# Hybrid decoder trunk: first modulation by blocks of 128 channels on TensorE, the first gate with it, sine tables early

## The chip, the cores and the metric

The kernel runs on one core of one Trainium2 chip. The metric is the device time of one execution in microseconds (us); the input arrays are laid out on the host beforehand and that does not count. A core has TensorE (PE; its weight loads are shown apart as PEld), VectorE (DVE), ScalarE (ACT), GpSimd (POOL) and SyncE (SP). SP and ACT issue the DMAs here, each in its own order. Engines take their instructions in order and wait for each other by semaphores.

## The reference

Two layers; 1024 tokens of 1024 channels; all in f32. Per layer:

```
c_act = silu(c)
shift, scale, gate = split(c_act @ w_mod + b_mod)            # 3 x 1024 channels
h = rms_norm(x, pre_gain) * (1 + scale) + shift
proj = h @ w_in                                              # 3088 columns
aq, ak, av, ag, rq, rk, rv, rg, gq, gk, gv, gg, ga = split(proj)
a = window_attention(rotary(aq), rotary(ak), av, sinks) * silu(ag)
r = rms_norm(retention(rotary(rq), rotary(rk), rv)) * silu(rg)
g = rms_norm(gated_linear_attention(gq, gk, gv, f(ga)), gain) * silu(gg)
y = concat(a, r, g) @ w_out
x = x + gate * rms_norm(y, post_gain)
```

The change is all in the start of layer 0: `c_act`, `shift` and `scale` of that layer, `h` of the first tokens, the columns `gg`, `ga` and `rg`, and the sines and cosines of `rotary`.

## The kernel before

Tokens go in eight tiles of 128. An f32 matrix product is made of three products of rounded parts: each operand is split into `hi` (rounded to fp32r) and `lo` (the rest), and hi*hi, lo*hi and hi*lo are summed in PSUM (`PASSES`, line 623). Weights come in units of 256 columns: four DMAs of 256 KB into staging tiles `st`, then for each a rounding (`hi`, ACT or DVE) and a subtraction (`lo`, DVE or POOL) into a slot of an arena (`load`, lines 523 to 563). The normalised and modulated tokens lie transposed, channels on partitions, as `hT`; a gate of one tile is 24 products, 8 blocks of channels times three passes (`project`).

*Order of the work.* PE takes its instructions in the order in which the program writes them (`manual_schedule` for PE, line 1770). Work beside the main line is written as generators, `job`s; a `yield` of a number asks to come on again when the planner's clock `clk` has gone on by so much, and `pump` writes what is due between the products. The waits in `L` (line 1729) are such due times. Instructions of the other engines, SP's and ACT's DMAs among them, are placed by the framework, where `issue_after` does not tie one to another.

*The start* (lines 246 to 350, 676 to 781). `c_act` needs one tanh on ACT. `mod_first` then takes the 8 MB of `w_mod` for shift and scale in two halves of 512 channels. Shift is summed on PE, 16 products with a weight of one column per half and pass; scale is summed on DVE, eight steps of 128x512 over a tile `acc`, then over the partitions on PE by one-column products (`finish`). Each half needs all 1024 rows of its columns, so the first half of the channels is known when half the weights are there. Meanwhile x of tiles 0 and 1 comes by the ACT queue, is squared, normalised (`xn`) and transposed into PSUM (`pre` with `early`); when a half of the modulation is known, ACT and DVE apply it in pieces of 128 channels and split the result. The weights of `gg` come between the two halves, x of tiles 2 and 3 and the weights of `rg` after them.

*Layer 0* (lines 1514 to 1541) goes over token pairs p: `gg` of p, then `rg` of p, for p from 0 to 3. `gg` also carries the 16 columns `ga` (272 columns in all). After the gates it goes over pairs again with `rq`, `rk` and `rv`. The sine tables are a job (`table_job`, line 1505): 16 steps over 128x512 on DVE and two sines on ACT, paced by `tb1` and `tb2` among the gates, then transposed and written to memory by `tables_T`, from where `rq` needs them.

PSUM has eight banks: three `mm` and five `aux`. SBUF tiles rotate by name: `t2` ten, `t1` eight, `st` five, `mx` two.

## Time and profile before

| | |
|---|---|
| median of three runs | 989.55 us (988.87 to 990.77) |
| profiled execution | 992.19 us |
| its span | 990.5 us |
| PE busy | 961.3 us, 97% |
| DVE, ACT, POOL busy | 694.1, 399.6, 246.5 us |
| granted PE clock, mean | 0.992 |

The profile is one execution; times in it run from the first instruction, and the time of an execution is its span and what lies around it. A row of the timeline gives the start, the time from the first to the end of the last, the engine, the line, the operation, the tile written and the tiles read, the sizes, how many, and in brackets the idle time of the engine before and what ended it. A group row (by line) gives the count, the busy time, the mean duration in ns, and the idle time before. An f32 product appears as two records, a product of rounded parts as one. L172 is the line of the helper through which every product goes, L187 that of the transposes; they are told apart by their tiles: `mm<-wm,c_act` is the modulation, `mm<-arena` and `mm<-arena,arena` products of tokens with weights (272 columns are `gg`, 256 others).

### The profile page before, as it was taken

Reading aid. Unit: us, or ns where it says so; the run is one execution under the profiler, and the core shown is the slowest. Engines: PE = TensorE matmul, PEld = TensorE weight load, DVE = VectorE, ACT = ScalarE, POOL = GpSimd, SP = SyncE. Lnnn points to the kernel's source line nnn. Section 1 sums busy time; section 2 is a strip of 40 time slices with the busy share of each in tenths; the row PEclk is TensorE's granted clock in tenths of the full one; section 3 lists DMA queues with packets and bytes.
Section 4 is the critical chain, followed back from the end, with each engine's and each line's share of the span. In section 5 each row is a group of like instructions: output and inputs, shape, how many; then the busy total and the mean of one; then the engine's idle time right before and its main releaser. Section 6 shows DMA issues by size and latency. Waiting matters only on the chain. (4 is left out here: it accounts for less than half of the span.)

```text
span 990.5 us, 19454 instructions
## 1 busy us (share of the span) xinstructions
PE 961.3 (97%) x7093; PEld 820.5 (83%) x7093; DVE 694.1 (70%) x1627; ACT 399.6 (40%) x1135; POOL 246.5 (25%) x310
## 2 busy tenths in 40 slices
PE   5899999999999999999999999999999999999996
PEld 1599999989998777778889999988999877777785
DVE  3798758778766787754687276785765577677886
ACT  2578301233332656633365321133333257664331
POOL 2232001223320224420124010123322034544100
PEclk8899999999999999999999999999999999999999
DMA  8844714443225354587665121342122434388883
GB/s 305 311 142 133 225 32 123 145 123 101 89 83 168 91 176 151 170 287 247 209 207 167 51 97 37 116 139 73 50 97 86 128 91 134 114 261 251 252 286 122
DMA packets 111056, 150.34 MB, mean 152 GB/s; under 512 B 12352, under 2 KB 60012, under 8 KB 110960
## 3 DMA queue, kind: packets, MB, share of 16 engines
q1 hardware_dynamic: 98928, 133.76, 43.0%
q10 hardware_dynamic: 12032, 15.33, 4.4%
q8 instruction: 56, 0.92, 0.4%
q14 instruction: 40, 0.33, 0.1%
HBM read 110.25 MB, written 36.70 MB: 148 GB/s over the span
## 5 line engine op out<-in xcount | busy, mean ns | idle before, releaser
L172 PE MATMUL mm<-arena 128*128 128x256 f32 (+2 forms) x1824 | 301.1, 318 | 2.3 <-ACT arena L726 1.8
L172 PE MATMUL mm<-arena,arena 128*128 128x256 f32 (+2 forms) x1824 | 297.2, 316 | 3.1 <-ACT arena L156 1.3
L172 PEld LDWEIGHTS mm<-arena 128*128 128x128 f32 x1824 | 255.1, 191 | 27.0 <-issue 4.2
L172 PEld LDWEIGHTS mm<-arena,arena 128*128 128x128 f32 x1824 | 251.6, 188 | 29.2 <-issue 6.1
L657 POOL TENSOR_TENSOR sm<-sm,mhalf 128x1 f32<-128x1 f32 (+1 forms) x64 | 58.9, 920 | 309.3 <-DVE sm L654 175.8
L172 PE MATMUL mm<-arena,mx 128*128 128x512 f32 (+1 forms) x564 | 130.8, 387 | 0.9 <-ACT kept L1389 0.9
L172 PEld LDWEIGHTS mm<-arena,mx 128*128 128x128 f32 x564 | 101.6, 188 | 25.0 <-issue 1.5
L156 ACT ACTIVATE t<-aux 128x256 f32<-128x256 f32 (+2 forms) x124 | 52.4, 437 | 89.9 <-PE aux L187 75.2
L156 ACT ACTIVATE arena<-st 128x512 fp32r<-128x512 f32 x94 | 56.2, 627 | 60.4 <-DMA st<-in_w_in_dram 25.4
L950 POOL TENSOR_TENSOR smx<-smx,sm 128x512 f32<-128x512 f32 x32 | 35.0, 1094 | 128.4 <-DVE sm L949 115.8
L548 POOL TENSOR_TENSOR arena<-st,arena 128x512 fp32r<-128x512 f32 x31 | 42.8, 1383 | 85.0 <-ACT arena L156 73.5
L548 DVE TENSOR_TENSOR arena<-st,arena 128x512 fp32r<-128x512 f32 x77 | 60.4, 802 | 2.9 <-ACT arena L156 1.7
L946 ACT ACTIVATE smx<-smx,sm 128x129 f32<-128x129 f32 x128 | 49.9, 393 | 29.7 <-DVE sm L943 29.6
L373 DVE SCALAR_TENSOR_TENSOR acc<-ms,c_act,acc 128x512 f32<-128x512 f32 x60 | 46.4, 774 | 20.1 <-DMA ms<-in_w_mod_dram 19.6
L187 PE MATMUL aux<-c_ident,t 128*128 128x128 f32 (+1 forms) x244 | 42.4, 286 | 7.3 <-DVE t L688 5.8
L994 ACT ACTIVATE t<-aux 128x256 f32<-128x256 f32 x32 | 12.2, 383 | 77.7 <-PE aux L172 71.7
L172 PEld LDWEIGHTS aux<-t,mx 32*128 32x128 f32 (+1 forms) x896 | 39.8, 187 | 3.8 <-issue 1.7
L187 PEld LDWEIGHTS aux<-c_ident,t 128*128 128x128 f32 (+1 forms) x244 | 30.0, 146 | 15.1 <-DVE t L688 7.6
L720 ACT ACTIVATE t<-aux,mod,mod 128x128 f32<-128x128 f32 x68 | 26.1, 458 | 39.7 <-PE aux L187 22.5
L172 PE MATMUL aux<-t,mx 32*128 32x32 f32 (+1 forms) x896 | 41.0, 272 | 0.0
L941 DVE COPY_PREDICATED smx<-c_curmask,aux 128x256 f32<-128x256 int32 x64 | 25.3, 446 | 17.1 <-ACT smx L156 14.0
L1296 DVE SCALAR_TENSOR_TENSOR t<-t,sm,t 128x512 f32<-128x512 f32 x32 | 24.2, 781 | 16.0 <-DMA t<-in_x_dram 9.3
(231 smaller groups left out, 1385.4 us busy)
## 6 DMA issues: line engine op xcount, KB each, us to landing
st<-in_w_in_dram SPq DMA_DIRECT2D x96, 256.0 KB, 3.7
ms<-in_w_mod_dram SPq DMA_DIRECT2D x64, 256.0 KB, 3.6
mx<-mixS SPq DMA_DIRECT2D x20, 512.0 KB, 5.2
st<-in_w_last_dram SPq DMA_DIRECT2D x36, 256.0 KB, 3.2
wm<-in_w_mod_dram SPq DMA_DIRECT2D x12, 512.0 KB, 6.2
t<-in_x_dram SPq DMA_DIRECT2D x24, 256.0 KB, 4.7
mixS<-t SPq DMA_DIRECT2D x40, 128.0 KB, 1.9
mixS<-t ACTq DMA_DIRECT2D x32, 128.0 KB, 2.0
```

What stands on the lines that cost most here:

```text
L156: A.activation(dst, src, AF.Copy)
L172: T.matmul(dst, lhsT, rhs, start=start, stop=stop)
L187: T.transpose(dst, src, idn)
L373: V.scalar_tensor_tensor(acc, wt, c_act[:, k:k + 1], acc, ALU.mult, ALU.add)
L548: e.tensor_tensor(lo, st, f(hi), ALU.subtract)
L657: G.tensor_tensor(r, r, mhalf[:, :w], ALU.pow)
L720: A.activation(hf[:, ks], at[kt], AF.Identity, scale=gain, bias=shift)
L941: V.copy_predicated(sv, curmask.unsqueeze(1).to_broadcast((P, 2, P)), pv[:, :, n // P - 1, :])
L946: A.activation(sm[:, h, :], sm[:, h, :], AF.Exp, bias=mx[:, h:h + 1], accum_out=sums[:, h:h + 1])
L950: eng("pn").tensor_tensor(sm[:, :, 0:128], sm[:, :, 0:128], rs.unsqueeze(2).to_broadcast((P, 4, P)), ALU.mult)
L994: A.activation(sq, po, AF.Square)
L1296: V.scalar_tensor_tensor(xt[j], yg[j], r, xt[j], ALU.mult, ALU.add)
```

## The change

The first stage is written anew, as `first_stage`, and inside it the instructions of all five engines keep their written order.

1. *Modulation by blocks.* The host lays the 8 MB out as eight blocks of 128 channels, shift and scale side by side (`w_m0`). For each block PE makes eight f32 products of 256 columns. Their weight is a column of `c_act` repeated 32 times, and they go in turn to four groups of 32 output partitions. ACT copies the sums to SBUF (`row`); two one-column products with a selector `sel` (1 on partitions 0, 32, 64, 96) add the four groups and turn the row into a column; DVE makes gain and shift. Nothing of this modulation is summed on DVE any more.
2. *x first.* x of tiles 0 to 3 comes ahead of the weights on SP. It is normalised in place. For each block four transposes fill one bank; gain and shift are applied to the four tiles by one ACT instruction, ACT rounds, DVE subtracts. In the last block ACT and DVE work from PSUM side by side.
3. *Gate block by block.* The `gg` products of four tiles (12 per block) are summed in four `aux` banks that stay open over the eight blocks; PE does those of block b-1 while block b is made. The weights of `gg` are converted, on ACT and POOL, after blocks 0, 2, 4 and 6, those of `rg` after block 7 (ACT, DVE, POOL).
4. *Sine tables early.* Their steps stand in DVE's order between the first steps of the stage (`more`): four ahead of the first tile, two after the squares of each tile, the rest after blocks 0, 1 and 2. The two sines come after block 1, and a tanh after block 2 brings ACT's table back. `table_job` goes.
5. *After it.* x of tiles 4 to 7 is asked for when the stage ends, into the tiles that held x of 2 and 3 and the table steps. Layer 0 goes on with `rg` of pairs 0 and 1, then `gg` and `rg` of 2, then of 3. The logits of tiles 0 to 3, the transposed tables and some constants (`late_consts`) are jobs after the stage; three due times are new.

```diff
-    A.activation(th0, c_nat, AF.Tanh, scale=0.5)
-    V.scalar_tensor_tensor(c_act, th0, 1.0, c_nat, ALU.add, ALU.mult)
-    V.tensor_scalar(c_act, c_act, 0.5, None, ALU.mult)
...
-    def mod_first(rws, between):
...
+    class Paced:
+        def __init__(self, issue, conv):
+            self.parts, self.todo, self.out = (issue, conv), list(range(4)), []
+        def issue(self):
+            kc = self.todo.pop(0)
+            self.out.append((kc, self.parts[0](kc)))
+        def convert(self):
+            kc, st = self.out.pop(0)
+            self.parts[1](kc, *st)
...
-                e = G if first == 0 or name[0] == "o" and kc == 2 else eng(f"wlo{kc}")
+                e = G if first == "AG" or name[0] == "o" and kc == 2 else eng(f"wlo{kc}")
...
+    def first_stage():
...
+        for t in range(4):
+            nc.sync.dma_start(xe[t], x_in[0, t * P:(t + 1) * P, :])
+        wm = bp.tile([P, 4 * SLOT], F32, tag="arena1", name="wm").rearrange("p (b k n) -> p b k n", b=KT, k=KT)
+        gg, rg = load(0, "gg", "AG"), load(0, "rg", "AV")
+        for b in range(KT):
+            for i in range(2):
+                nc.sync.dma_start(wm[:, b, 4 * i:4 * i + 4], w_m0[b, :, 4 * i:4 * i + 4].rearrange("p k j n -> p k (j n)"))
+            if b in (0, 2, 4, 5):
+                gg.issue()
+        for _ in range(4):
+            rg.issue()
...
+        V.tensor_copy(posf, pposf[:, 0:8])
+        more(1)
+        A.activation(th0, c_nat, AF.Tanh, scale=0.5)
+        V.scalar_tensor_tensor(c_act, th0, 1.0, c_nat, ALU.add, ALU.mult)
+        V.tensor_scalar(c_act, c_act, 0.5, None, ALU.mult)
+        more(2)
+        rc = [mod_rows_t(r_) for r_ in rws]
...
+        more(1)
+        for t in range(4):
+            ss = squares([xe[t][:, 512 * j:512 * j + 512] for j in range(2)], [t2(), t2()])
+            r = rstd2(ss)
...
+            more(2)
+            V.tensor_scalar(xe[t], xe[t], r, None, ALU.mult)
+        acc = [aux() for _ in range(4)]
+        pm = aux()
...
+        for b in range(KT):
+            last = b == KT - 1
+            at = mm()
+            for t in range(4):
+                transp(at[:, t * P:(t + 1) * P], xe[t][:, b * P:b * P + P], ident)
+            for k in range(KT):
+                g = k % 4
+                mult(pm[32 * g:32 * g + 32, 0:256], c_act[:, k:k + 1].to_broadcast((P, 32)), wm[:, b, k], k < 4, k > 3, 0.11)
+            row = t1()
+            A.activation(row, pm[:, 0:256], AF.Copy)
+            if b and not last:
+                products(b - 1, (0, 1))
+            c0 = 256 + 2 * b
+            for j in range(2):
+                mult(pm[:, c0 + j:c0 + j + 1], row[:, j * P:(j + 1) * P], sel, True, True)
+            V.scalar_tensor_tensor(gain[:, b:b + 1], pm[:, c0 + 1:c0 + 2], base[:, b:b + 1], rc[1][:, 8 + b:9 + b],
+                                   ALU.add, ALU.mult)
+            V.tensor_tensor(shift[:, b:b + 1], pm[:, c0:c0 + 1], rc[0][:, b:b + 1], ALU.add)
...
+            if last:
+                A.activation(hi, av, AF.Identity, scale=gain[:, b:b + 1], bias=shift[:, b:b + 1])
+                V.tensor_scalar(hf, at, gain[:, b:b + 1], shift[:, b:b + 1], ALU.mult, ALU.add)
+            else:
+                A.activation(hf, at, AF.Identity, scale=gain[:, b:b + 1], bias=shift[:, b:b + 1])
+                A.activation(hi, hv, AF.Copy)
+            V.tensor_tensor(lo, hv, f(hi), ALU.subtract)
+            if b:
+                products(b - 1, range(4) if last else (2, 3))
+            if b % 2 == 0:
+                gg.convert()
+            if b == 0:
+                more(2)
+            elif b == 1:
+                more(1)
+            elif b == 2:
+                more(2)
+                A.activation(th0, c_nat, AF.Tanh, scale=0.5)
+        arenas.append(bp.tile([P, 4 * SLOT], F32R, tag="arena1", name="arena1"))
+        for _ in range(4):
+            rg.convert()
+        products(KT - 1, range(4))
+        for xt in x_pair() + x_pair():
+            nc.sync.dma_start(xt, x_in[0, (4 + len(late)) * P:(5 + len(late)) * P, :])
+            late.append(xt)
...
+    with tc.manual_schedule(engines={getattr(mybir.EngineType, e) for e in FIXED}):
+        first = first_stage()
...
+        if l == 0:
+            for name, p in (("rg", 0), ("rg", 1), ("gg", 2), ("rg", 2), ("gg", 3), ("rg", 3)):
+                do_gates(name, p)
...
-L = {... "tt1": 7.12, ... "tb1": 12.59, "tb2": 0.89, ... "pf3": 11.64, "pf1": 6.18, "pf2": 5.11, ...}
+L = {... "tt1": 18.0, ... "pf3": 0.3, "pf2": 2.6, ...}
...
+    inputs["w_m0"] = np.asarray(inputs["w_mod"])[0, :, :2 * D].reshape(P, KT, 2, KT, P).transpose(3, 0, 1, 2, 4)
```

`products(b, ts)` writes, for each tile of `ts`, hi*hi, hi*lo and lo*hi of block b into that tile's bank; `more(n)` takes n steps of the tables.

More of the change, by code (lines that the diff above doesn't have):

```diff
@@ L772, in trunk @@
-    with tc.tile_pool(name="first", bufs=1) as wp:
-        mod_first(rws, between)
-    ap = ctx.enter_context(tc.tile_pool(name="big1", bufs=1))
-    arenas.append(ap.tile([P, 4 * SLOT], F32R, name="arena1"))
-    with tc.issue_after(mark[0].ins), tc.issue_after(mark[3].ins):
-        for t in (2, 3):
-            job(pre(0, t, xe[t], soon=True))
-        pump()
-    with tc.issue_after(mark[0].ins), tc.issue_after(mark[1].ins):
-        load(0, "rg", 1)
-    for t in range(4, NT):
-        job(pre_first(t))
@@ L1502, in last_output @@
             pump()
[L1505 to L1512 removed]
     def layer(l):
[L1515 to L1517 removed]
+        if l:
+            new_ga()
         def do_gates(name, p):
@@ L1718, in layer @@
         load(l + 1, "rq")
+    new_ga()
+    for t in range(4):
+        job(gla_logits(0, t, first[t][:, 0:256], first[t][:, 256:272]))
+    job(gla_log(0, 0))
+    job(tables_T())
+    job(late_consts())
+    late_x()
     for l in range(DEPTH):
```

252 lines of the change are left out of this document (96 added, 156 removed).

## The prediction

> **What bounds the kernel now.** I read the page first, then the stretches of the span, then the timeline of PE.
>
> ```profile
> PE 961.3 (97%) x7093; PEld 820.5 (83%) x7093; DVE 694.1 (70%) x1627; ACT 399.6 (40%) x1135; POOL 246.5 (25%) x310
> ...
> 0.00:19.00 19.00, 8.34 (x16) 1.46 (x17) 5.28 (x16) 4.38 (x10) 1.76 (x10) 0.97 0.85 283
> 19.00:25.00 6.00, 5.12 (x18) 3.21 (x19) 3.27 (x8) 1.89 (x3) 3.89 (x5) 0.52 1.04 379
> 25.00:38.00 13.00, 12.58 (x55) 5.75 (x53) 8.20 (x17) 6.07 (x15) 3.35 (x4) 1.00 1.04 395
> 38.00:46.00 8.00, 6.19 (x31) 6.06 (x30) 6.90 (x20) 4.89 (x14) 1.79 (x4) 0.57 0.76 240
> ...
> 70.00:120.00 50.00, 47.56 (x392) 46.20 (x390) 43.20 (x94) 28.85 (x63) 9.74 (x13) 1.00 0.59 171
> 120.00:990.50 870.50, 857.96 (x6397) 734.58 (x6394) 605.39 (x1419) 336.00 (x983) 216.54 (x262) 1.00 0.45 142
> ```
>
> The columns after the stretch are busy PE, weight loads, DVE, ACT, POOL, granted clock, DMA share and GB/s. PE is the bound from about 46 us on. What the start costs is when PE reaches a given amount of gate work; from there the end moves with it. The timeline of PE gives that moment.
>
> ```profile
> 39.94 6.05 PE L172 MATMUL mm<-arena 128*128 128x272 f32 x27 [1.81 <-ACT arena L726]
> 45.83 1.04 PE L187 MATMUL aux<-c_ident,t 128*128 128x128 f32 x8
> ...
> 50.41 5.82 PE L172 MATMUL mm<-arena,arena 128*128 128x256 f32 x48
> 56.06 1.92 PE L172 MATMUL mm<-arena 128*128 128x272 f32 x14
> ...
> 57.85 3.27 PE L172 MATMUL mm<-arena 128*128 128x272 f32 x24
> ```
>
> At 56.06 the kernel has 48 `gg` and 48 `rg` products and the transposes of four tiles behind it. The changed kernel has 96 `gg` products when its first stage ends. So I compare its end with 56.06. A product of 272 columns starts every 0.13 us (24 in 3.27, less the last one's tail) and one of 256 every 0.12; 48 wider ones done early leave 0.6 us less to do.
>
> **The start of the new stage.** Nothing of it can run on PE before the four x tiles are normalised, and DVE now issues in written order: twelve steps of the sine tables stand ahead of and between the scalings.
>
> ```profile
> 5.39 0.22 DVE L414 CAST posr<-posi 8x128 f32<-8x128 int32 x1 [4.46 <-DMA posi<-in_positions_dram]
> ...
> L433 DVE SCALAR_TENSOR_TENSOR mx<-mx 128x512 f32<-128x512 f32 x4 | 2.7, 686 | 0.0
> ...
> L662 DVE TENSOR_TENSOR sm<-sm 128x1 f32<-128x1 f32 x8 | 1.2, 154 | 1.4 <-ACT t L673 1.4
> ...
> L425 DVE TENSOR_TENSOR mx<-sm,c_freq 128x512 f32<-128x512 f32 x1 | 0.7, 684 | 0.0
> ...
> L435 DVE TENSOR_SCALAR mx<-mx 128x512 f32<-128x512 f32 x1 | 0.4, 420 | 0.0
> ...
> L673 ACT ACTIVATE t<-xk 128x512 f32<-128x512 f32 x4 | 2.5, 629 | 10.6 <-DMA t<-in_b_mod_dram 6.5 <-DMA xk<-in_x_dram 4.0
> ```
>
> The positions let DVE begin at about 6.1. Until the fourth scaling it does: the angle (0.7), two steps for `c_act` (0.4), seven three-operand steps (0.72 each with the gap, 5.0), four one-input steps (0.45 each, 1.8), small copies and sums (0.5), four times the two steps of the root (0.35, 1.4), the low part of the 16 columns (0.3) and four scalings over 1024 columns (0.42 for 512 columns, of which 0.15 is what one column takes: 0.7 each, 2.8). Sum 12.9, so 19.0; one transpose more and block 0 is transposed at 19.3. POOL's power lies beside the table steps. ACT's squares (8 of 0.63, 8 reads of an estimated 0.2, from about 6, after nine DMA issues and a table load) end by 13, and x is there by 10: 2.1 MB at the 283 GB/s of the first stretch. The modulation weights do not bind: x, weights and `gg` are 11.5 MB, at 283, then 379 to 395 GB/s in by 35, and block 7 is multiplied at 50.
>
> **One block.** Four transposes, eight f32 products with 32 columns of weights in four column groups (16 records), two one-column sums (4 records), twelve gate products.
>
> ```profile
> 18.86 1.97 PE L187 MATMUL aux<-c_ident,t 128*128 128x128 f32 x8 [4.44 <-DVE t L688]
> ...
> 27.71 1.05 PE L172 MATMUL mm<-c_ones,t 128*128 128x1 f32 x8
> ...
> 29.67 5.31 PE L172 MATMUL mm<-wm,c_act 128*1 128x512 f32 x12
> ...
> 226.14 0.32 PE L172 MATMUL aux<-t,t 128*32 128x64 f32 x8
> 226.39 1.34 PE L172 MATMUL mm<-arena 128*128 128x256 f32 x9
> ```
>
> A 512-column f32 record takes 0.44 at full clock (5.31 / 12), so 256 columns 0.22. Side by side in fours the 16 records cost 0.9; one after the other 3.5. The row at 226.14 has just this shape, four column groups, and its eight records fit into 0.25 before the next product starts, where two rounds of 64 columns would be 0.11 and eight records in turn 0.44. I take 0.9; the other end would add 2.6 a block, 21 us in all. [...]
>
> With transposes 0.5 (four at 1.04 / 8), sums 0.5 (1.05 / 8 each) and half the gate products 0.8 (six at 0.13), a block is 0.5 + 0.9 + 0.5 + 1.6 = 3.5 of PE at full clock. At half clock the transposes are 1.0 (1.97 / 8 each), the others by the same doubling 1.8 and 1.0, and a gate product is 0.22 (27 in 6.05). What other engines put between one block's sums and the next block's comes from these rows.
>
> ```profile
> L1011 ACT ACTIVATE t<-mm 128x256 f32<-128x256 f32 x16 | 6.1, 383 | 0.5 <-PE mm L172 0.5
> ...
> L542 ACT ACTIVATE arena<-st 128x512 fp32r<-128x512 f32 x4 | 2.5, 626 | 3.0 <-DMA st<-in_w_in_dram 3.0
> ...
> L461 ACT ACTIVATE t<-aux 128x512 f32<-128x512 f32 x2 | 1.2, 589 | 0.0
> ...
> 27.29 1.29 POOL L548 TENSOR_TENSOR arena<-st,arena 128x512 fp32r<-128x512 f32 x1 [0.67 <-ACT arena L542]
> ...
> 40.53 0.68 DVE L730 TENSOR_TENSOR arena<-t,arena 128x512 fp32r<-128x512 f32 x1
> ...
> 77.54 1.28 ACT L446 ACT_TABLE_LOAD   x1
> 79.46 0.64 ACT L446 ACTIVATE sincos<-mx 128x512 f32<-128x512 f32 x1 [0.64 <-DVE mx L442]
> 80.00 0.61 ACT L447 ACTIVATE sincos<-mx 128x512 f32<-128x512 f32 x1
> ```
>
> After the sums: gain and shift 0.3, ACT modulates 0.6 and rounds 0.6 (1.5 so far), DVE's low part 0.7. PE meanwhile has 0.8 + 0.5 + 0.9 = 2.2 to do, so the chain is hidden. On even blocks ACT then rounds a quarter of `gg` (0.6) and POOL makes its low part (1.3): ready 3.4 after the sums, and the second gate product of the next block needs it, 1.2 later than PE does. After block 1 the sine table load and two sines (1.3 + 1.2) stand on ACT ahead of the next row copy (0.4); after block 2 the way back to tanh (1.5).
>
> Times at which the sums end: block 0: 19.3 + 1.8 + 0.4 + 1.0 = 22.5. Block 1: the low weights are there at 25.9, products 0.7, sums 0.5: 27.1, about when the clock is full. Block 2: 27.1 + 1.5 + 2.5 + 0.4 + 0.5 = 32.0. Block 3: 32.0 + 1.5 + 0.6 + 1.5 + 0.4 + 0.6 = 36.6. Block 4: +3.5 = 40.1. Block 5: 40.1 + 3.4 + 0.7 + 0.5 = 44.7. Block 6: 48.2. Block 7: row copy behind the last rounding, 51.3. Then 12 products of block 6 (low weights at 51.6) to 53.1 and 12 of block 7 to 54.7. Against 56.06, and with the 0.6: **1.9 us gained.** What the change removes (the products on DVE, the 32 one-row records, the half-clock stretch from 38 to 46) lies before 56.06 and is counted with it.
>
> **What is moved behind.** x of tiles 4 to 7 waits on SP until block 7 is transposed (50 instead of 38), lands from 53 on (0.5 MB each 1.4 us), and the transposes of tile 4 are planned 7.7 after the stage (`pf3` 0.3 and `pre1` 7.44), 63 with PE a little slower than the planner's clock. ACT has `rg`'s four roundings (to 54.7), four gates (2.3) and squares (1.6), then root and scaling 2: ready at 61. It costs nothing with 2 us to spare; without that cover it would cost PE what it is late. `rg`'s weights: ACT done at 54.7, POOL's part at 56.1, PE needs that at 56.7. The constants queue on SP behind x. The gate matrix is the first of them that PE reads, some 20 us after the stage by the planner's `gz1` and `gz2` (10.94 and 9.73), so they cost nothing.
>
> The tables leave the later stretch: 9.5 us of DVE (nine steps of 0.69, the angle 0.7, six one-input steps of 0.42 to 0.6), 1.2 of sines and two table loads. These PE waits stand there.
>
> ```profile
> 75.01 1.66 PE L172 MATMUL mm<-arena,arena 128*128 128x272 f32 x10 [0.62 <-ACT arena L726]
> ...
> 82.38 1.79 PE L172 MATMUL mm<-arena 128*128 128x256 f32 x13 [0.48 <-DVE t L1013]
> ...
> 111.56 0.50 PE L172 MATMUL mm<-arena,arena 128*128 128x256 f32 x2 [1.14 <-ACT arena L156]
> 112.26 0.97 PE L172 MATMUL mm<-arena,arena 128*128 128x256 f32 x6 [0.20 <-ACT arena L156]
> ...
> 81.99 1.28 ACT L1011 ACT_TABLE_LOAD   x1
> ...
> 102.19 1.85 SPq L473 DMA_DIRECT2D tabA<-t  x4
> 104.09 0.43 SPq L161 DMA_DIRECT2D st<-in_w_in_dram  x1
> ```
>
> The wait at 82.38 follows the return of the tanh table; it should go, and so should the one at 75.01 (tiles come earlier against their use). The 1.3 at 111 to 112 is weights issued at 104 behind table writes on SP, which now go sooner; I take half. Sum 0.6 + 0.5 + 0.7 = 1.8, bounds 0 and 2.4. The planner's clock also shifts the slots of later jobs. After 120 PE is idle for 12.5 us in all (870.50 - 857.96); no row says which way that goes, so I take 0 and 2 either way.
>
> **Sum.** 1.9 + 1.8 = 3.7. The profiled execution took 992.19 with a span of 990.5 and lies 2.6 above the median of 989.55. 992.19 - 3.7 = 988.5 for such an execution, 986.0 (rounded up from 985.9) against the median.
>
> **Rivals.** *Nothing holds the blocks* (0.18): weights and tables hide, as POOL's row at 27.29 does beside PE today. Then PE alone counts: 22.5 + 1.0 + 1.8 + 0.8 + 0.5 = 26.6 for block 1, six blocks at 3.5, 3.2 of products: 50.8, a gain of 5.3 + 0.6 and 2.4 later, 981. Against it: the order on ACT and POOL is written out, and nothing else there is ahead of these steps that could move.
>
> *The stage stays at half clock, slower* (0.24). For it: the trace was at 0.52 from 19 to 25 and again at 0.57 from 38 to 46, after a stretch of one-column products and a 1.8 wait, and was kept there for nearly 6 us of products (the row at 39.94). The new stage begins idle and has waits of 1 us at each even block and at the tables. At half clock throughout, a block is 3.8 + 2.7 and the stage ends at 71, 14.3 late with the 0.6; less 1.8, that is 1002. Each us at half clock beyond 25 costs 0.5: after 7 the gain is gone, after 11 it is slower by over 0.2%. Against it: in between PE is over 75% busy. [...]
>
> *No difference* (0.16): the stage ends at 56.5 and the weights at 111 still wait: 989.5. For it: the tables are hidden beside PE today, and here they cost 7.5 us (5.0 + 1.8 + 0.7) of DVE ahead of block 0.
>
> **Chances.** My forecast 0.42. About 2 us (0.2%) is what a measurement can tell here. Faster by more: the first rival 0.18 and most of the forecast, 0.56 in all; within: 0.18; slower 0.26 (half clock and shifted slots). Range 979 to 995: both rivals that end early and half of the clock's. My own case alone: 983 to 990.
>
> **What would show it.** Fourth scaling at 19 on DVE; sums every 3.5 and 4.6 us in turn; PE's waits on POOL's weights after even blocks and on ACT after blocks 1 and 2; full clock from 25 on; last product of the stage at 54.7; no table load at 77 and 82, no wait at 111. I am wrong if the clock row from 25 to 55 is below 0.9, if PE waits for tile 4, or if a block takes over 5.

## The result and the profile after

The changed kernel is slower: 996.16 us (median, 993.95 to 996.82) against 990.19 for the kernel before on the same chip. The ratio is 1.0053, with a 95% interval of 1.0037 to 1.0069. I had forecast 986.0 with a range to 995. The profiled execution took 993.95 us with a span of 992.2, against 992.19 and 990.5 before, so the two profiles show only 1.8 of the 6 us.

The stretches of the span of the changed kernel, with the same columns as before:

```profile
0.00:19.00 19.00, 2.22 (x6) 1.08 (x6) 11.81 (x34) 6.86 (x19) 4.64 (x14) 1.00 0.85 282
19.00:25.00 6.00, 5.46 (x37) 2.94 (x41) 0.48 (x3) 2.03 (x4) 0.00 (x0) 1.00 1.03 416
25.00:38.00 13.00, 11.90 (x81) 8.32 (x73) 5.30 (x10) 7.77 (x12) 2.14 (x2) 1.00 0.84 339
38.00:46.00 8.00, 7.38 (x72) 5.69 (x72) 3.29 (x8) 4.72 (x10) 0.48 (x2) 1.00 0.10 34
...
70.00:120.00 50.00, 45.66 (x377) 44.90 (x376) 41.40 (x96) 28.11 (x69) 10.70 (x14) 1.00 0.65 188
120.00:992.20 872.20, 861.93 (x6439) 739.97 (x6438) 607.25 (x1425) 339.93 (x986) 216.62 (x262) 1.00 0.46 143
```

Two things are seen. In 70 to 120 PE is busy 45.66 us, where it was 47.56. And the clock column prints 1.00 from the start, which is wrong for the first rows: this trace has no record of the clock before 33.6, where full clock begins, so the clock ahead of it has to be read from equal products. PE's timeline of the first stage shows it:

```profile
19.43 1.94 PE L172 MATMUL aux<-wm,c_act 128*32 128x256 f32 x16
21.88 1.01 PE L172 MATMUL aux<-sm,t 128*128 128x1 f32 x4 [0.51 <-ACT t L750]
...
31.20 1.94 PE L172 MATMUL aux<-wm,c_act 128*32 128x256 f32 x16
...
34.16 0.50 PE L172 MATMUL aux<-sm,t 128*128 128x1 f32 x4
...
35.89 1.07 PE L172 MATMUL aux<-wm,c_act 128*32 128x256 f32 x16
...
38.48 0.90 PE L172 MATMUL aux<-arena 128*128 128x272 f32 x5 [0.97 <-POOL arena L502]
...
47.26 0.89 PE L172 MATMUL aux<-arena 128*128 128x272 f32 x5 [0.95 <-POOL arena L502]
...
58.48 1.52 PE L172 MATMUL aux<-arena 128*128 128x272 f32 x10 [0.55 <-DVE arena L768]
59.84 9.53 PE L172 MATMUL mm<-arena,arena 128*128 128x256 f32 x79
```

The same 16 records of a block take 1.94 us in blocks 0 to 2 and 1.07 from block 3 on: half clock until between 33 and 34 us, which agrees with the first record. `rg` starts at 59.84, where the forecast had 54.7 and the kernel before had the same amount of gate work done at 56.06. Behind the stage there are two long waits. The first is new. The second, on a rounding of the weights of `rv` (L158, DVE), stands ahead of the same products as the 1.14 and 0.20 at 111.56 and 112.26 in the kernel before, which were waits for ACT:

```profile
72.17 0.60 PE L187 MATMUL aux<-c_ident,ga 128*48 128x128 f32 x4
75.08 0.65 PE L187 MATMUL aux<-c_ident,mx 128*128 128x128 f32 x4 [2.30 <-ACT t L654]
...
116.62 4.80 PE L172 MATMUL mm<-arena,arena 128*128 128x256 f32 x38 [2.01 <-DVE arena L158]
...
220.93 0.44 PE L187 MATMUL aux<-c_ident,t 128*128 128x128 f32 x2 [0.45 <-ACT t L1147]
```

Before, at the last of these places, which is the same place of the program:

```profile
215.79 0.44 PE L187 MATMUL aux<-c_ident,t 128*128 128x128 f32 x2 [0.43 <-ACT t L1126]
```

The account closes at 221: 59.84 - 56.06 is 3.8 late, less the 0.6 of wider products already done 3.2; the waits of 60 to 120 are 2.30 + 2.01 = 4.3 in place of 2.4 (0.62 + 0.48 + 1.14 + 0.20), 1.9 more. 3.2 + 1.9 = 5.1, and 220.93 - 215.79 is 5.1. The lag stays for long: the same transposes come at 642.5 against 637.6 (4.9 late) and at 775.6 against 771.3 (4.4 late). At the end it is 1.7, and there the kernel before has waits of 0.87 (at 928) and 1.08 (at 941) in its profile that the changed one lacks. That is not the rule, as the next run of the same kernel shows.

### The profile page after: what moved, and what is told of

It is laid out like the page before. It is cut to its first block, busy times and chain, and to the rows that moved or that the text cites. A ratio compares the mean times of both kernels' runs of the same rounds, so it can differ in the third digit from the quotient of the medians.

```text
span 992.2 us, 19621 instructions
## 1 busy us (share of the span) xinstructions
PE 956.4 (96%) x7189; PEld 822.4 (83%) x7189; DVE 682.5 (69%) x1604; ACT 403.2 (41%) x1133; POOL 244.2 (25%) x310
## 4 chain that ended last, share of the span: by engine, by line
PE 81%; DVE 8%; issue 4%; DMA 3%; POOL 2%; ACT 1%; POOLq 0%; SPq 0%; DVEq 0%; ACTq 0%
PE mm L172 60%; PE aux L172 17%; PE aux L187 4%; DMA t<-in_x_dram 1%; POOL sm L610 1%; DMA ms<-in_w_mod_dram 1%; POOL arena L502 1%; DVE acc L321 0%; DVE t L656 0%; DVE t L1317 0%; DVE t L1210 0%; DVE t L1212 0%; ACT t L654 0%; DMA c_ones<-cst_ones_dram 0%; DMA t<-in_pre_norm_gain_dram 0%
## 5 line engine op out<-in xcount | busy, mean ns | idle before, releaser
L172 PE MATMUL mm<-arena 128*128 128x256 f32 (+2 forms) x1728 | 284.9, 318 | 0.0
L172 PEld LDWEIGHTS mm<-arena 128*128 128x128 f32 x1728 | 240.4, 189 | 24.3 <-issue 4.2
L187 PE MATMUL aux<-c_ident,t 128*128 128x128 f32 (+1 forms) x180 | 32.4, 277 | 4.4 <-DMA t<-in_pre_norm_gain_dram 2.6
L172 PEld LDWEIGHTS aux<-kT,mx 64*128 64x128 f32 x384 | 24.6, 185 | 10.9 <-issue 6.3
L1020 DVE TENSOR_TENSOR t<-aux,sm 128x256 f32<-128x256 f32 x32 | 13.6, 425 | 27.4 <-POOL sm L610 27.4
```

The source lines that it names most:

```text
L172: T.matmul(dst, lhsT, rhs, start=start, stop=stop)
L187: T.transpose(dst, src, idn)
L1020: V.tensor_tensor(h4(g1), h4(po), r.unsqueeze(2).to_broadcast((P, 4, 64)), ALU.mult)
```

## The experiments

Each kernel is the changed one with the edit named; the kernel before ran beside it on the same chip. The ratio is of all their runs, with its 95% interval, and need not be the quotient of two medians. "rg" is when the first product after the stage starts, "waits" PE's waits of over 0.14 us from there to 120, summed, both from the kernel's own profile.

| kernel | us | ratio to before | rg | waits |
|---|---|---|---|---|
| the changed kernel again | 995.21 | 1.0056 [1.0041, 1.0070] | 59.26 | 4.3 |
| extra products | 996.12 | 1.0057 [1.0031, 1.0083] | 59.75 | 4.0 |
| low parts on DVE | 996.10 | 1.0061 [1.0046, 1.0076] | 58.24 | 5.3 |
| tables not in the fixed order | 1007.92 | 1.0186 [1.0171, 1.0201] | 60.80 | 6.7 |
| extra products, low parts on DVE | 996.91 | 1.0060 [1.0036, 1.0083] | 56.02 | 5.0 |
| later logits | 993.13 | 1.0012 [0.9997, 1.0028] | 62.27 | 1.9 |
| rv on ACT and POOL | 993.69 | 1.0027 [1.0012, 1.0043] | 60.36 | 2.3 |
| tables behind the stage | 1010.23 | 1.0181 [1.0149, 1.0212] | 54.48 | 8.7 |
| later logits, rv | 993.45 | 1.0021 [1.0004, 1.0038] | 60.76 | 1.5 |
| the same, low parts | 992.19 | 1.0012 [0.9994, 1.0029] | 57.73 | 2.5 |
| the same, extra products | 991.59 | 1.0017 [0.9995, 1.0038] | 56.29 | 2.5 |
| the same, rq asked for later | 994.95 | 1.0060 [1.0045, 1.0076] | 56.37 | 6.1 |
| that without extra products | 994.90 | 1.0050 [1.0036, 1.0064] | 57.83 | 5.3 |
| all four, rq on ACT and POOL | 993.87 | 1.0034 [1.0021, 1.0047] | 55.89 | 2.9 |
| that without extra products | 991.34 | 1.0007 [0.9994, 1.0021] | 58.15 | 2.9 |
| one bank for ga | 996.05 | 1.0065 [1.0050, 1.0081] | 59.18 | 3.7 |
| one bank, low parts, rq, rv | 994.01 | 1.0040 [1.0025, 1.0056] | 57.93 | 3.7 |
| that with extra products | 993.37 | 1.0042 [1.0025, 1.0059] | 55.93 | 3.8 |

**The changed kernel again.**

> The changed kernel once more, as the base for the three others on the same chip. Expected 1.005 of the kernel before, and a first stage that again ends near 59.8 us with products at half speed until about 33. If the half-speed stretch has another length in this execution, the end of the stage moves by half of the difference.

The same code, and another profile: the wait at 114 is followed by a spell at half clock, and the span is 995.0, 4.5 longer than that of the kernel before.

```profile
116.07 6.28 PE L172 MATMUL mm<-arena,arena 128*128 128x256 f32 x38 [2.03 <-DVE arena L158]
```

```profile
117.00:121.00 4.00, 4.00 (x24) 4.00 (x23) 3.44 (x6) 0.00 (x0) 0.00 (x0) 0.57 0.52 159
```

The same 38 products took 4.80 us in the first profile and 6.28 here. So a wait of 2 us can cost 1.5 more, or not; one profile is one draw.

**Is it the clock?** 24 products of the identity with itself, read by nobody (`WARM` is 8, 5, 5, 6), ahead of and between block 0's transposes; then the low parts of `gg` on DVE in place of POOL; then both.

```diff
+                if b == 0:
+                    for _ in range(WARM[t]):
+                        T.matmul(wb[:, 0:P], ident, ident, start=True, stop=True)
```

```diff
-                e = G if first == "AG" or name[0] == "o" and kc == 2 else eng(f"wlo{kc}")
+                e = V if first == "AG" else G if name[0] == "o" and kc == 2 else eng(f"wlo{kc}")
```

> 24 useless f32 products of the identity with itself stand on PE ahead of and between the four transposes of block 0, from about 9 to 19 us; nothing reads their result. Theory A (PE starts the stage at half speed and stays there to 33, and that is the main loss): block 0's eight modulation products take 0.7 us from first to last start instead of 1.3, the sums of block 3 end 4.4 us earlier, the stage ends at about 55.4 instead of 59.8, the time falls by 4 us (0.4%). Rival B (the chain through ACT, DVE and POOL sets the pace of the blocks, PE's speed is hidden): the stage ends within 1 us of 59.8 and the time stays.

> The low parts of gg's weights in the first stage are made on DVE (0.69 us) instead of POOL (1.27 us). Theory C (POOL's part holds the second gate product after each even block): the waits of 0.97 and 0.95 us after blocks 2 and 4 fall to about 0.4, and the one after block 6 goes; the stage ends 1.5 to 2 us earlier and the time falls by as much. Rival: something else is there at the same moment and the stage ends within 0.5 us.

> Both earlier edits of the first stage at once: 24 extra products of c_ident with itself on PE ahead of and between block 0's transposes, and the low parts of the gg weights on DVE in place of POOL. Theory (half clock in the blocks sets the stage's end, and it comes back only because PE waits about 0.95 us on POOL after each even block): the eight f32 products of a block take 0.69 us in all eight blocks, rg starts at 53 to 55 in place of 59.8, 5 to 7 us earlier; of this at least half reaches the end, 990 to 993. Rival (the later waits take all of it, as they took the 1.5 us of the run with low parts on DVE alone): rg starts as early, the waits on the five aux banks and on the rv weights grow by the same amount, 995 to 996.

With the extra products alone the clock is full in block 0 (its 16 records take 1.07), but it falls again behind the waits on POOL, three times (26.6, 36.9 and 47.1, each for 3.4 us at a recorded 0.5, and there the 16 records take 1.66 to 1.73). `rg` starts as late as the rival said. The first of these waits:

```profile
23.92 0.39 PE L172 MATMUL aux<-arena 128*128 128x272 f32 x1 [0.92 <-ACT arena L498]
25.26 0.90 PE L172 MATMUL aux<-arena 128*128 128x272 f32 x5 [0.95 <-POOL arena L502]
...
28.63 1.73 PE L172 MATMUL aux<-wm,c_act 128*32 128x256 f32 x16
```

Low parts on DVE alone shorten the waits after blocks 2 and 4 to 0.42, as expected, and `rg` starts 1.6 earlier (58.24). The time does not fall with it: there are a new wait of 1.17 at 81.44 and two spells at half clock, at 73 and 117 (0.52 and 0.51 granted).

With both edits the waits for the low parts are 0.41 and the blocks run at full clock throughout in this execution (16 records in 1.07 in all eight):

```profile
19.64 1.07 PE L172 MATMUL aux<-wm,c_act 128*32 128x256 f32 x16
...
25.08 0.89 PE L172 MATMUL aux<-arena 128*128 128x272 f32 x5 [0.41 <-DVE arena L502]
...
30.97 0.61 PE L172 MATMUL aux<-sm,t 128*128 128x1 f32 x4 [1.23 <-ACT t L754]
...
56.02 4.24 PE L172 MATMUL mm<-arena,arena 128*128 128x256 f32 x34
...
79.09 0.64 PE L172 MATMUL mm<-arena,arena 128*128 128x272 f32 x3 [0.91 <-ACT arena L660]
115.01 6.29 PE L172 MATMUL mm<-arena,arena 128*128 128x256 f32 x38 [1.82 <-DVE arena L158]
```

The sums of the blocks now end at 21.8, 26.3, 31.6, 36.4, 40.2, 44.7, 48.4 and 51.8, all within 0.8 of the forecast (22.5 to 51.3), and `rg` starts 3.8 earlier than in the changed kernel. That agreement is in part luck: the waits for the low parts are 0.41 here and were forecast at 1.2, and `rg` is still 1.3 behind 54.7. Of the 3.8, low parts on DVE bring 1.6 alone and the extra products 2.2 on top of them, but only 0.1 alone. So the clock is shown to cost the stage some 2 us where POOL does not hold it, and the rest is argued. Nor does a spell of 3.4 us at half clock always cost its 1.7: in the four later kernels with both edits one spell of 3.4 us stands in the stage (0.96 granted over 19 to 60 in two of them), and `rg` starts at 55.89 to 56.37 all the same.

The time stays at 1.0060. The waits after the stage are all still there, a new one of 0.91 beside them, and this profile has two spells at half clock in 72 to 120 (0.5 recorded, 3.4 us each). The place that the changed kernel reaches at 121.25 is reached at 121.14: of the 3.8 nothing is left. The rival's outcome came, though not as it said, for the two old waits did not grow.

**Tables.** The steps of the tables from the second on taken out of the stage, at first simply out of its order, then tied behind its last low part (`held[0]`); a job steps through them as in the kernel before:

```diff
+        with tc.issue_after(held[0].ins):
+            V.tensor_scalar(nn, ang, 1.0 / (TWO_PI * 4096.0), MAGIC, ALU.mult, ALU.add)
...
-        more(1)
+        next(sin)
+        table.append(sin)
```

> The steps of the sine tables, all but the first, run after the stage with the due times they had in the kernel before; the tanh after block 2 goes. (The tables work inside the memory of their result, so x of tiles 4 and 5 has its buffer sooner.) Theory D (the tables are 6.8 us of DVE ahead of block 0 and 2.5 + 1.5 us of ACT inside blocks 1 and 2): the fourth scaling ends at 12.5 to 14 instead of 19, the stage ends at 51 to 53 instead of 59.8; after it 1 to 2 us of PE waits come back between 60 and 95; the time falls by 5 to 7 us, to about that of the kernel before. Rival (weights or the clock hold the stage anyway): the stage ends after 57 and the time falls by less than 2 us.

> The steps of the sine tables from the second on, and the two sines, stand on DVE and ACT behind the stage's last low part (tied to it), in the tiles sincos itself, paced by a job as in the kernel before; block 2's second tanh goes with them. Theory (the steps ahead of block 0 delay the stage one for one): the fourth scaling ends at 13 to 15 in place of 19, rg starts at 54 to 56; the table loads and the tables' writing come back to 65 to 105, with waits of 1 to 4 us there. Rival (the stage is held by the clock and the weights, not by its start): rg starts at 58 or later although the fourth scaling ends at 15 or earlier.

The first of the two decides nothing about the stage: freed from the written order, the steps were placed between the same scalings as before, and both sines stood at 18. In the second the fourth scaling ends at 16.6 and `rg` starts at 54.48, 5.4 earlier. It is nevertheless as slow as the first of the two (1.0181), with these waits:

```profile
15.89 0.75 DVE L731 TENSOR_SCALAR mx<-mx,sm 128x1024 f32<-128x1024 f32 x1 [0.66 <-POOL sm L611]
```

```profile
69.63 0.27 PE L187 MATMUL aux<-c_ident,ga 128*48 128x128 f32 x1 [2.27 <-DVE t L657]
72.20 1.11 PE L187 MATMUL aux<-c_ident,mx 128*128 128x128 f32 x4 [2.30 <-ACT t L655]
107.01 0.79 PE L172 MATMUL aux<-gaT,gwt 128*128 128x512 f32 x1 [4.17 <-ACT gaT L1058]
```

Two readings. Without the 7.5 us of table steps the scalings end only 2.3 earlier, because POOL's root (0.66 of wait ahead of the scaling) then sets their pace. And the earliest end of the stage of all runs goes with one of the two worst times: here too it is the stretch after the stage that decides. Its waits are only half of that. The place that the kernel before reaches at 215.79 comes at 231.04, 15.3 late, though PE leaves the stage 2.2 ahead (with the 0.6). The waits to 120 are 6.3 more than the 2.4 of before, and another of 1.58 stands at 131. The granted clock is 0.87 over 60 to 112 and 0.93 over 112 to 140; by an estimate from these, 0.13 of 52 and 0.07 of 28 us, half clock behind the waits cost 8.7 us more, about as much as the waits.

**The two waits.** The first logits of tiles 0 to 3 due 8 us later; the weights of `rv` of layer 0 rounded on ACT, with low parts on POOL; both.

```diff
-        yield lat("gz1", l)
+        yield lat("gz1", l) + (8.0 if l == 0 and t < 4 else 0.0)
```

```diff
+                elif l == 0 and name == "rv":
+                    A.activation(hi, st, AF.Copy)
...
-                e = G if first == "AG" or ...
+                e = G if l == 0 and name == "rv" else G if first == "AG" or ...
```

> The first gate logits of the four first tiles in layer 0 are due 8 us later; nothing else is changed. Theory (the four ga transposes at 72 take four of the five aux banks while ACT is behind, and tile 5's transposes then wait): the wait of 2.30 us at 72.8 is gone, 2 to 4 us faster than the changed kernel, 992 to 994. Rival (PE is ahead of ACT at that place in any case): a wait of about 2 us on ACT stands within 10 us of there, 995 to 996.5.

> The weights of rv in layer 0: their rounding on ACT (in part on DVE in the changed kernel), the low parts on POOL; nothing else is changed. Theory (the first rounding at 116.05 waits on DVE behind the rotary steps of 108.9 to 116): the wait of 2.01 us at 114.6 is gone, and with it the half clock that followed it in two of the three runs with it (117.5 to 121, 1.7 us): 992 to 994. Rival (the staging tiles or ACT are late too): a wait of over 1 us remains at the start of rv, 995 to 996.5.

> The two edits after the stage together: the first logits of tiles 0 to 3 due 8 us later, and the weights of rv of layer 0 rounded on ACT with the low parts on POOL. Theory (the two waits are separate, each with its own cost of about 2 us and a spell of half clock behind it): the gains of the single edits add, 3 to 4.5 us below the changed kernel, 990.5 to 992.5, level with the kernel before. Rival (the later of the two is only moved by the earlier): as the better of the single edits, 993 to 994.

PE's timeline with later logits, then with `rv` moved:

```profile
84.10 0.69 PE L187 MATMUL aux<-c_ident,ga 128*48 128x128 f32 x2 [0.56 <-DVE t L656]
85.69 0.27 PE L187 MATMUL aux<-c_ident,ga 128*48 128x128 f32 x1 [0.91 <-ACT gaT L1050]
```

```profile
115.01 4.71 PE L172 MATMUL mm<-arena,arena 128*128 128x256 f32 x38
```

Each edit removes its wait. Later logits take back over half of the loss and `rv` about half: 1.0012 and 1.0027 against 1.0056 for the changed kernel, by the medians 2.2 and 2.8 us above the kernel before against 5.2. The intervals of the first and of the changed kernel are apart; those of the second and of the changed kernel overlap by 0.0002. In the profile with later logits `rg` starts at 62.27, later than in any other kernel, with two spells at half clock in the stage (0.995 granted over the whole execution). That execution took 993.58, 2.7 above the median of the kernel before, and PE is still 5.1 late in it at the place of 642; so its profile does not show the gain that the ratio over all runs has. With later logits the wait at 114 has also fallen, to 0.24, which may be why the gains do not add: together the edits give 1.0021. The rival of the pair (as the better of the two) is nearer.

**Does an earlier stage then count?** The two edits and low parts on DVE; then the extra products too.

> The same two edits and the low parts of the gg weights on DVE in place of POOL. Theory (the 1.5 us that low parts on DVE alone gave at the stage's end were eaten by these two waits): with the waits away it reaches the end, 989 to 991. Rival (other waits, or the clock, take it again): 991 to 993.

> The same three edits and the 24 extra products of c_ident with itself ahead of block 0. Theory (the stage's end, 3.8 us earlier with the last two of these edits, counts in full once the two later waits are away): 986 to 989, below both kernels. Rival (tiles 4 to 7 or the weights come too late for a stage that ends at 56, so new waits stand between 60 and 120): 990 to 993.

1.0012 and 1.0017: the stage ends 3.0 and 4.5 earlier than with the two edits alone, and the time does not follow. In both, a new wait of 2.23 has come up with a spell at half clock behind it (0.97 granted over 60 to 120), in the second one here:

```profile
72.82 1.43 PE L172 MATMUL mm<-arena,arena 128*128 128x272 f32 x6 [2.23 <-DVE arena L663]
```

```profile
69.82 1.61 DVE L158 CAST arena<-st 128x512 fp32r<-128x512 f32 x1 [1.72 <-DMA st<-in_w_in_dram]
...
72.08 1.29 DVE L663 TENSOR_TENSOR arena<-t,arena 128x512 fp32r<-128x512 f32 x2
```

DVE rounds the first weights of `rq`, not needed until some 30 us later, ahead of tile 4's low part, which PE waits for. So I asked for them later (after `rg` of pair 1), and, when that failed, left the request and gave the rounding to ACT and the low parts to POOL, each with and without the extra products.

```diff
-                if name == "rg" and p == 0:
+                if name == "rg" and p == 1:
                     load(l, "rq")
```

```diff
-                elif l == 0 and name == "rv":
+                elif l == 0 and name in ("rq", "rv"):
```

> The four edits of the run before (extra products ahead of block 0, low parts of gg on DVE, later logits, rv on ACT and POOL), and rq's weights asked for after the gates rg of pair 1 in place of pair 0. Theory (the new wait of 2.23 us at 70.6 and the half clock behind it come from the rounding of rq's weights, which stands on DVE between tile 4's modulation and its low part at 69.8 to 71.5): the wait falls under 0.7 us, the clock stays full there, PE enters the part after 216 some 3 to 4 us earlier, 987 to 989. Rival (rq's weights are then late for their own use near 100, or the next wait grows): a wait of over 1.5 us stands between 75 and 120, 990.5 to 993.

> As the last one without the 24 extra products ahead of block 0. Theory (what the clock costs in the blocks still counts when the later waits are away): 1 to 2 us slower than with them, 988.5 to 990.5, its rg starting 1 to 2 us later. Rival (the slack after the stage takes it): the two are equal within 0.5 us.

> The four edits (extra products ahead of block 0, low parts of gg on DVE, later logits, rv on ACT and POOL), with rq's weights asked for where they were, but rounded on ACT with the low parts on POOL as those of rv. Theory (the wait of 2.23 us at 70.6 comes from the rounding of rq's first weights on DVE ahead of tile 4's low part): the wait falls under 1 us, the clock stays full behind it, PE enters the part after 216 some 2 to 4 us earlier: 987.5 to 989.5, below both kernels. Rival (ACT is the late engine there, with one rounding more): a wait of 1.5 us or more on ACT between 66 and 80, 991 to 994.

> As the last one without the 24 extra products ahead of block 0. Theory (the clock in the blocks costs the end what it costs the stage once the later waits are away): 1 to 2 us slower than with them, 989 to 991. Rival (they give nothing at the end): equal within 0.5 us.

Asked for later, the weights are late for their own use:

```profile
107.69 0.39 PE L172 MATMUL mm<-arena 128*128 128x256 f32 x1 [1.93 <-ACT arena L156]
111.29 3.56 PE L172 MATMUL mm<-arena 128*128 128x256 f32 x28 [1.57 <-DVE arena L504]
```

With ACT and POOL, the wait becomes 0.80 and the logits wait 1.90 for ACT, so that the sum is 2.9:

```profile
76.69 1.52 PE L172 MATMUL mm<-arena,arena 128*128 128x272 f32 x10 [0.80 <-ACT arena L662]
82.52 0.27 PE L187 MATMUL aux<-c_ident,ga 128*48 128x128 f32 x1 [1.90 <-ACT t L656]
```

Without the extra products that is the best of all, 1.0007 [0.9994, 1.0021]: level with the kernel before, not below it. With them it is 1.0034, although `rg` starts 2.3 earlier. Neither the theory nor the rival of that pair allowed for this.

**One bank.** I had put the wait at 72.8 down to the five `aux` banks. To test that, the four ga transposes went into one bank at their old time: alone, with the edits for `gg`, `rq` and `rv`, and with the extra products too (now written into block 0's own bank).

```diff
-        pt = aux()
-        transp(pt[0:48, 0:P], f(g3).rearrange("p a n -> p (a n)"), ident)
+        if l == 0 and 0 < t < 4:
+            pt = gapt[0]
+        else:
+            pt = gapt[0] = aux()
+        q = t * P if l == 0 and t < 4 else 0
+        transp(pt[0:48, q:q + P], f(g3).rearrange("p a n -> p (a n)"), ident)
```

> The changed kernel, with one edit: the four ga transposes of tiles 0 to 3 go into one PSUM bank in place of four. Their time is not moved. Theory (the banks are what tile 5's transposes wait for): the wait of 2.30 us at 72.8 falls under 0.5 us, 2 to 3 us below the changed kernel, 992.5 to 994.5. Rival (ACT is late there whatever the banks): a wait of over 1.5 us on ACT stays between 70 and 80, 995 to 996.5.

> Low parts of gg on DVE, rq and rv of layer 0 rounded on ACT with low parts on POOL, the four ga transposes in one bank at their old time (not 8 us later). Theory (banks): no wait over 0.8 us between 60 and 120, 988 to 990. Rival: a wait of 1.5 us or more on ACT near 70 to 75, 991 to 993.

> The last one, with the 24 extra products of c_ident with itself ahead of block 0 written into block 0's own bank, so that the banks rotate as without them (in the three earlier combined runs they had a bank of their own, and waits of 1.3 to 1.8 us at 654 and 0.98 to 1.5 at 728 that the runs without them lack). Theory (the stage's half clock counts at the end, and those late waits came from the shifted banks): 1 to 2 us below the last one, 986.5 to 988.5, and no wait over 0.8 at 654. Rival: the late waits return and the two are equal.

```profile
74.62 0.27 PE L187 MATMUL aux<-c_ident,ga 128*48 128x128 f32 x1 [2.84 <-ACT gaT L1056]
75.34 0.38 PE L187 MATMUL aux<-c_ident,ga 128*48 128x128 f32 x1 [0.45 <-ACT gaT L1056]
```

Within one bank each transpose waited until ACT had copied the one before it, 2.84 for the first copy and 0.45 for each after it. The edit brought its own wait, so it does not tell the banks from ACT. It does show that ACT's copy comes 2.8 us after PE is ready at that place. Whether more banks would have helped is open.

The last pair gives the fullest account of the stage's clock. `rg` starts 2.0 earlier with the extra products (55.93 against 57.93), PE is 2.1 ahead near 218 and 1.3 at 658, and the medians differ by 0.6. The rows without and with them:

```profile
219.78 0.44 PE L187 MATMUL aux<-c_ident,t 128*128 128x128 f32 x2 [0.45 <-ACT t L1155]
658.53 2.74 PE L172 MATMUL mm<-arena,arena 128*128 128x256 f32 x21 [0.77 <-DVE t L1221]
```

```profile
217.66 0.44 PE L187 MATMUL aux<-c_ident,t 128*128 128x128 f32 x2 [0.45 <-ACT t L1158]
657.26 2.75 PE L172 MATMUL mm<-arena,arena 128*128 128x256 f32 x21 [1.65 <-DVE t L1224]
```

At 657 PE waits for the rotary steps on DVE, 0.9 longer with the extra products. The same longer wait (1.3 to 1.8, against at most 0.8 in the changed kernels without them) stands there in every kernel with extra products, whatever bank they use, so my guess that their bank was the cause fell. That PE comes earlier is not the cause either: with extra products and low parts PE is at the place of 642.5 just when the changed kernel is, and waits 1.80 where that waits 0.56. DVE's timeline, without and with them, shows where the wait comes from:

```profile
643.39 0.75 DVE L321 SCALAR_TENSOR_TENSOR acc<-ms,c_act,acc 128x512 f32<-128x512 f32 x1 [1.04 <-DMA ms<-in_w_mod_dram]
```

```profile
642.59 0.75 DVE L321 SCALAR_TENSOR_TENSOR acc<-ms,c_act,acc 128x512 f32<-128x512 f32 x1 [2.40 <-DMA ms<-in_w_mod_dram]
```

DVE waits for the weights of another modulation (`ms`) and is then late for the rotary steps. In all six kernels with extra products this wait is 2.0 to 2.7; in every other kernel no wait of DVE for these weights there is over 1.14. Why they land later is open. So the lead that the extra products give is kept for 500 us and lost there: in all six pairs it is 0.8 to 2.3 at the place of 121, 0.8 to 2.2 at that of 642, and between -1.9 and 1.3 at that of 734 (all by the changed kernel's times).

## Why the prediction was wrong

*Yardstick (56.06 against the end of the stage).* It held as a measure of PE's lag: 3.2 behind plus 1.9 of waits is the 5.1 at 221, and 4.4 of it is left at 776. In every kernel of the table but the two on tables, the lag at the place of 121 is still there within 0.41 at that of 642. It is the last 200 us that differ between executions: from 4.4 to 1.7 late in the first profile, from 5.3 to 4.5 in the second. Against the forecast, PE is 8.8 late at 221: 5.1 of them are the stage, 3.7 the waits.

*Start.* The fourth scaling was forecast to end at 19.0 and ended at 18.97 (18.23 + 0.74). But the sum over DVE was not the only bound: with 7.5 us of it taken out, the end came 2.3 earlier.

*One block.* The records held: 16 cost 1.07 to the end of the last, 0.9 forecast; side by side, not in turn. The waits after even blocks were 0.97 and 0.95 (forecast 1.2). The blocks as a whole were a little longer than their sum: at full clock in the changed kernel the sums of blocks 2 to 6 end at 34.7, 39.7, 43.5, 48.5 and 52.2, steps of 5.1, 3.8, 5.0 and 3.8 where 4.6, 3.5, 4.6 and 3.5 were forecast.

*The clock, the first step that failed.* I took full clock from 25 to 27 on; it came at 33.6. By the second rival's own price, 0.5 per us, that makes 3 to 4 us. The stalls of the table load and the tanh were covered by the slow blocks, and with the cover gone one shows (1.23 at 30.97). So the stage was 2.7 late at the first sums at full clock (block 2, 34.7 for 32.0). The rest of the 5.1 came at full clock: 1.7 from the longer blocks (block 7's sums at 55.7 for 51.3) and 0.8 in the products behind them. The experiment gives the clock 2.2. My test by the clock's row could not have shown it, since the row prints 1.00 there.

*What is moved behind, the second step that failed.* x of tiles 4 to 7, the constants and the table loads went as said. But I booked -1.8 for waits that go, bounds 0 and -2.4, and did not ask what would be late next. The waits went from 2.4 to 4.3, +1.9, outside the bounds on the other side. The two that I expected to go (0.62 and 0.48) went. New is the first of the two: squares and modulation of tiles 4 to 7 stand on ACT at the time when the four ga transposes come. And the 1.3 at 111, of which I booked half, became 2.0. The roundings on ACT that were late there are in time now (the third ends at 112.3). But the first quarter of `rv`, which DVE rounds in both kernels, was rounded at 99.31 before, ahead of the rotary steps on DVE (104.24 to 111.2), and is now rounded at 116.05, behind them (108.89 to 116.1); its weights are asked for at 104.27, before at 75.52. By the ratios, the edit that removes the first wait (and leaves 0.24 of the second) takes back 0.44% and the one that removes the second 0.29% of 0.56% (by the medians 3.0 and 2.4 of 5.2 us). So these waits are about half of the loss or more. With both gone 1.0021 is left, and PE is 3.1 late at the place of 121 in that profile (119.26 against 116.14 before): that is the stage.

*After 120.* Taken as 0 and 2 either way: PE's idle time went from 12.5 to 10.3 (872.20 - 861.93), just outside, to the good; in the second profile it is 11.95 (875.00 - 863.05).

*Rivals.* Neither came as priced. "Half clock, slower" had the right place and price, and the outcome was on its side. But over the kernels of the table the time does not go with the stage's end: the earliest `rg` (54.48) is among the slowest, the latest (62.27) belongs to one of the best ratios. The ratio goes with the waits between 60 and 120 (correlation 0.87 over the eighteen rows; -0.15 with the start of `rg`; 0.83 and -0.23 without the two rows on tables). That is an association over edits that I chose, and each `rg` and each sum of waits is from one execution. The six pairs with and without extra products do not show that an early end is worth nothing: their lead lasts to 642 and is lost by a wait that comes with the extra products themselves.

*Open.* What full clock in the stage would be worth at the end without that side effect (the medians of the pairs differ by 0.6 in its favour at most, with 1 to 2 us of uncertainty each), why the modulation weights land later with extra products, and whether banks or ACT alone make the wait at 72.8. No version here is faster than the kernel before.

## What to carry to other kernels

Work moved out of a start has to go somewhere: list for the stretch behind it what each engine will hold at each time, before booking its old waits as gains. A stage that begins on an idle PE, with small waits in each step, should be priced at half clock until shown otherwise (here 16 equal records took 1.94 us in the first three blocks and 1.07 after), and the clock read from equal products, not from a mean. And follow an earlier arrival through the trace: compare the times of the same place of the program early, in the middle and late, make one late wait shorter, then look for where the time comes back before the next edit.

## What was not expected of the hardware

*Half clock behind short waits.* With the extra products, waits of 0.92 and 0.95 us within 24 to 26 us were followed by 16 records in 1.73 in place of 1.07. With 0.93 and 0.41 at the same place they were not, and in another kernel with nearly the same two waits (all four edits, `rq` on ACT and POOL) they were:

```profile
24.18 0.39 PE L172 MATMUL aux<-arena 128*128 128x272 f32 x1 [0.92 <-ACT arena L498]
24.99 0.89 PE L172 MATMUL aux<-arena 128*128 128x272 f32 x5 [0.42 <-DVE arena L504]
...
28.07 1.94 PE L172 MATMUL aux<-wm,c_act 128*32 128x256 f32 x16
```

So the length of these waits alone does not decide it. With low parts on DVE alone, waits of 2.28 and 1.82 were each followed by a spell of about 3.4 us:

```profile
73.00:76.50 3.50, 3.05 (x14) 3.06 (x15) 2.71 (x6) 2.75 (x10) 1.79 (x2) 0.52 0.79 151
...
117.50:121.00 3.50, 3.50 (x18) 3.50 (x19) 3.43 (x6) 0.00 (x0) 0.00 (x0) 0.51 0.29 91
```

In the first profile of the changed kernel the same two waits (2.30 and 2.01) brought none: the clock is 1.00 over 72 to 76.5 and over 117 to 121. So waits of 2 us, and twice 0.9, were followed by half clock in some executions and not in others. What decides it was not shown.

*Full clock came 14 us after block 0's products began* (19.43 to 33.6). PE was busy 5.46 of 6.00 and 11.90 of 13.00 us from 19 to 38 and reached full clock only at 33.6. With 24 extra products before block 0 it was there before 20 (a record of full clock from 13.0 on, and block 0's 16 records in 1.07 at 19.29). How much work it takes was not shown.

*A rounding on DVE took 1.61 us* for 128x512, where another took 0.42 (116.05, changed kernel), while POOL filled a tile from 69.35 to 71.16:

```profile
116.05 0.42 DVE L158 CAST arena<-st 128x512 fp32r<-128x512 f32 x1
```

```profile
69.35 1.81 POOL L832 MEMSET mx<- 128x2048 f32 x1 [4.40 <-PE aux L187]
```

Over all traces of this case, eleven roundings of this size on DVE took 0.78 to 1.61, and each of them began while an instruction of POOL ran and ended 0.28 to 0.31 after that instruction's end. The 452 with nothing on POOL beside them took at most 0.43. Some others that began beside POOL were not slowed, and no experiment tried it by itself, so when it happens is open.

*Transposes into one bank waited for the copy of another part of it* (2.84 for the first copy, 0.45 for each after it, with one bank for ga). The trace shows this order and these waits; what makes the transposes wait was not tried.
